# A two-block token mixer on one core: slot buffers moved by 96 bytes, four small moves between GpSimd and VectorE around a recurrence, and a longer lead of gates in the merge behind it

## The chip, the cores and the metric

The kernel runs on one core of a Trainium2 chip. The metric is the device time of one execution in microseconds. Three executions of the kernel before took 3236.25, 3236.37 and 3238.22 us; their median is 3236.37 us.

## The reference, cut to what matters

Four layers are applied one after the other to 512 tokens of width 1024 in float32: two layers of a first block, then two of a second. What matters here is the second block:

```
h = rmsnorm(x, pre_norm_g)
proj = h @ w_in
y_b = attention(...) * silu(z_b)
y_c = rg_lru(x_c, ...) * silu(z_c)            # 1280 channels
y_a = gmlp(...) * silu(z_a)
merged = sigmoid(g_a)*(y_a @ w_proj_a) + sigmoid(g_b)*(y_b @ w_proj_b) + sigmoid(g_c)*(y_c @ w_proj_c)
x = x + rmsnorm(merged @ w_out, post_norm_g)

rg_lru:  xc = conv4(x_c) + b
         r, i = sigmoid(blockdiag(xc, w_a) + b_a), sigmoid(blockdiag(xc, w_x) + b_x)   # 16 blocks of 80
         a = exp(-8 r softplus(-lam));  h_t = a_t h_{t-1} + sqrt(1 - a_t^2) * i_t * xc_t
```

## The kernel before, in words

**Arithmetic.** Every float32 matrix product is made of three products of fp32r halves: each operand is split into a high part (a rounded copy, made by ScalarE) and a low part (the rest, made by VectorE). `mm3` (lines 322 to 324) issues high times high, high times low, low times high. Most of these are 128x128 stationary by 512 columns moving.

**Weights.** All weights lie in HBM in the order in which they are used, as chunks of 128x1024. SyncE loads pairs of chunks into `raw`; `Stream._split` makes `whi` (ScalarE, line 179) and `wlo` (VectorE, line 180) from them, four chunks ahead of their use, in rings of seven.

**Activations.** The normalised input lies in two fixed tiles `hh` and `hl`. Everything else of 128x512 lies in 48 slots of 2048 bytes, which the trace calls `s`; `Slots.t` takes the slot that has been free the longest. `projT` makes one 128x512 output tile: eight blocks of a weight against `hh`/`hl` (24 matmuls), or as many as a list of slot pairs has. In `out_proj`, `tok_proj` and the attention the slots or `hh` are the stationary operand and the weights move.

**Where the buffers lie.** The tiles of a partition are laid one behind the other: `ident` (512 bytes), `pv` (2880), `half` (rounded up to 32), `hh` and `hl` (16384 each), the seven `whi` and seven `wlo` (4096 each), two `raw` (8192 each), the pool `small`, and the 48 slots. From `hh` to the end of `raw` each size is a multiple of 4096. The pool `small` holds, each tile rounded up to 32 bytes, 24 tiles of 32 bytes, 3 of 96, 3 of 64, 3 of 512, one of 256 and one of 192: 3232 bytes, which is 25 times 128 and 32.

**The recurrence (`lru`).** Ten tiles m of 128 channels. An iteration takes the gate weights of tile m+1 (`gate_weights`), makes the convolution of tile m+3 (`conv`, lines 1123 to 1130), copies rows that a block of 80 has outside its tile into a packed tile with DMAs (`pack`, line 1146, on the queues of GpSimd and SyncE), in four iterations (`ZPOS`: 4, 6, 7, 8) makes a projection z, and makes the two gates (`gates`). For six of the ten tiles the packed rows stand as high, low, high, so that one matmul of 96 rows (line 1170) does what otherwise takes three; it needs 32 rows of low weights beside the high ones, and the small copy on line 1160 puts them there: two per such tile, 24 in both layers. Behind the gates comes the product of the gate i with xc (line 1177). `scan` (lines 1185 to 1199) runs in pieces between these steps, at each `tick`: exponentials and square roots on ScalarE, a product (1196) and the scan itself (1197) on VectorE. After the tenth tile the remaining z projections follow, and for each tile silu(z) (lines 941, 942), its product with h (1238, or 1248 for the last two) and the split of the result (306, 307).

**The merge.** `merge` computes two gate tiles (`gate(0)`, `gate(1)`) ahead, and then, for each of eight outputs m, the projection of the branch's result, its product with the gate and the sum into `acc` (lines 683, 688), and `gate(m + 2)`.

**Order.** All of it is one program order written by hand: each engine runs its instructions in the order of the code. Each instruction waits only for what it reads and for buffers that it overwrites.

Of the kernel before, what the change touches and what calls it, by code (L numbers as in the profile page):

```python
# [8 lines left out]
F32 = mybir.dt.float32  # L9
F32R = mybir.dt.float32r  # L10
AF = mybir.ActivationFunctionType
ALU = mybir.AluOpType
# [5 lines left out]
KD = D // 128  # L18
# [15 lines left out]
E_U, E_V, E_ZA, E_CQ, E_CKV, E_KR, E_ZB, E_XC, E_ZC, E_GA, E_GB, E_GC = (  # L34
    0, 1024, 2048, 3072, 3456, 3712, 3776, 4800, 6080, 7360, 8384, 9408)

LW = 1280
NLT = LW // 128
# [41 lines left out]
def lru_rows(m):  # L80
    rows = [128 * k + i for k, r0, r1 in lru_outside(m) for i in range(r0, r1)]
    return tuple(rows * 3 if 3 * len(rows) <= 128 else rows)
# [27 lines left out]
class Slots:  # L110
    def __init__(self, pool, n, tag):
        self.pool, self.tag = pool, tag
        self.free_ = deque(range(n))
        self.where = {}
        self.low = n
        self.cnt = 0
# [121 lines left out]
class Kernel:  # L238
    def __init__(self, nc, tc, ctx, aps, total):
        self.nc, self.tc = nc, tc  # L240
        self.x_in, self.w, self.pv_in, self.rows, self.gmw, self.cst, self.out = aps
        fixed = ctx.enter_context(tc.tile_pool(name="fixed", bufs=1))
        self.wp = ctx.enter_context(tc.tile_pool(name="wp", bufs=RING))
        self.rawp = ctx.enter_context(tc.tile_pool(name="rawp", bufs=RAW))
        self.sm = ctx.enter_context(tc.tile_pool(name="small", bufs=6))
        self.s = Slots(ctx.enter_context(tc.tile_pool(name="slots", bufs=1)), NSLOT, "s")
        self.p = Slots(ctx.enter_context(tc.tile_pool(name="psum", bufs=1, space=bass.MemoryType.PSUM)), 8, "p")
        self.ws = Stream(self, total)
        self.ident = fixed.tile([128, 128], F32, tag="ident", name="ident")
        self.pv = fixed.tile([128, PV["n"]], F32, tag="pv", name="pv")  # L250
        self.half = fixed.tile([128, 4], F32, tag="half", name="half")
        self.hh = fixed.tile([128, KD, S], F32R, tag="hh", name="hh")
        self.hl = fixed.tile([128, KD, S], F32R, tag="hl", name="hl")
        self.xd = tc.dram_tile((S, D), F32, name="xd")
        self.h_op = [Op(self.hh[:, k, :], self.hl[:, k, :]) for k in range(KD)]
        self.lanes = {}
        self.x_src = self.x_in
        self.pend = None
        self.ht = {}
        self.pre = {}  # L260
        self.x = {}
# [399 lines left out]
        out[h] = self.split(sg[h])  # L661
        yield

    def merge(self, l, wg, cg, wy, ops, acc, n_br, last):

        nc, s, p = self.nc, self.s, self.p
        out, sgs = {}, {}

        def gate(m):
            pg = self.projT(wg, l, cg + 128 * m)  # L670
            sgs[m] = s.t()
            nc.scalar.activation(sgs[m][:], pg[:], AF.Sigmoid)  # L672
            p.f(pg)
            self.tick()

        gate(0)
        gate(1)
        if callable(ops):
            ops = ops()
        for m in range(KD):  # L680
            sg = sgs.pop(m)
            py = self.projT(wy, l, 128 * m, op=ops)
            nc.vector.tensor_tensor(sg[:], py[:], sg[:], op=ALU.mult)  # L683
            p.f(py)
            if n_br == 0:
                acc[m] = sg
            else:
                nc.vector.tensor_tensor(acc[m][:], acc[m][:], sg[:], op=ALU.add)  # L688
                s.f(sg)
                if last:  # L690
                    out[m] = self.split(acc.pop(m))
            self.tick()
            if m + 2 < KD:
                gate(m + 2)
        for o in ops:
            s.f(o.hi, o.lo)
        return out
# [402 lines left out]
    def lru(self, l):  # L1100
        nc, s, p = self.nc, self.s, self.p
        tt = nc.vector.tensor_tensor
        xc, op = {}, {}
# [30 lines left out]
        rr, ii, pk = {}, {}, {}  # L1134
# [17 lines left out]
        def gate_weights(m):  # L1152

            n = len(lru_rows(m))
            for nm in ("lru_w_a_2", "lru_w_x_2"):
                a = ws.take(128, (nm, l, 128 * m, 128 * m))
                hi, lo = ws.take(128, (nm, l, lru_rows(m), 128 * m))
                if n % 3 == 0 and n <= 96:
                    k = slice(n // 3 * 2, n)
                    nc.vector.tensor_copy(hi[k], lo[k].bitcast(F32))  # L1160
                gw[nm, m] = (a, (hi, lo))

        def gates(m):
            n, tiles = pk.pop(m)
            for nm, bias, dst in (("lru_w_a_2", "lba", rr), ("lru_w_x_2", "lbx", ii)):
                a, (hi, lo) = gw.pop((nm, m))
                ps = p.t()
                self.mm3(ps[:], a, (op[m].hi[:], op[m].lo[:]), True, False)
                if len(tiles) == 1:
                    nc.tensor.matmul(ps[:], hi[0:3 * n], tiles[0][0:3 * n, :], start=False, stop=True)  # L1170
                else:
                    self.mm3(ps[:], (hi[0:n], lo[0:n]), (tiles[0][0:n, :], tiles[1][0:n, :]), False, True)
                t = s.t()
                nc.scalar.activation(t[:], ps[:], AF.Sigmoid, bias=self.col(bias, l, m))
                p.f(ps)
                dst[m] = t
            nc.gpsimd.tensor_tensor(ii[m][:], ii[m][:], xc[m][:], op=ALU.mult)
            o = op.pop(m)
            s.f(xc.pop(m), o.hi, o.lo, *tiles)
            self.tick()  # L1180
# [26 lines left out]
        pack(1)  # L1207
        pz, sz = {}, {}
        gate_weights(0)
        for m in range(NLT):  # L1210
            if m + 1 < NLT:
                gate_weights(m + 1)
            if m + 3 < NLT:
                conv(m + 3)
                pack(m + 2)
                if m + 3 == NLT - 1:
                    pack(NLT - 1)
            if m in ZPOS:
                z = len(sz) + len(pz)
                ps = self.projT("w_in_2", l, E_ZC + 128 * z)  # L1220
                if m < 8:
                    sz[z] = self.silu(ps)
                else:
                    pz[z] = ps
                self.tick()
            gates(m)
            if m == 3:
                self.lane("scan", scan(range(4)))
        self.drain("scan")
        self.lane("scan", scan(range(4, NLT)))  # L1230
        ops = []
        nz = len(sz) + len(pz)
        for z in range(nz, NLT):
            pz[z] = self.projT("w_in_2", l, E_ZC + 128 * z)
            self.tick()
            for m in range(len(ops), z - 1):
                t = sz.pop(m) if m in sz else self.silu(pz.pop(m))
# [8 lines left out]
        for t in rest:  # L1246
            m = len(ops)
            tt(t[:], t[:], h[m][:], op=ALU.mult)
            s.f(h.pop(m))
            ops.append(self.split(t, eng=nc.gpsimd if m == NLT - 2 else None))  # L1250
        return ops

    def gmlp(self, l):
# [67 lines left out]
    def block2(self, l, last=False):  # L1321
        s = self.s
        c = self.mla_down(l)
        zb = []
        for h in range(3):
            ps = self.projT("w_in_2", l, E_ZB + 128 * h)
            if h == 0:
                self.tick()
            zb.append(self.silu(ps))
            if h:  # L1330
                self.tick(3)
        self.drain("mla")
        self.mla(l, c, zb)

        def yb():
            return [z if isinstance(z, Op) else self.split(z) for z in zb]

        acc = {}
        self.merge(l, "w_in_2", E_GB, "w_proj_b_2", yb, acc, 0, False)
        yc = self.lru(l)  # L1340
        self.merge(l, "w_in_2", E_GC, "w_proj_c_2", yc, acc, 1, False)
        ya = self.gmlp(l)
        self.x_load()
        merged = self.merge(l, "w_in_2", E_GA, "w_proj_a_2", ya, acc, 2, True)

        def done(k):
            s.f(merged[k].hi, merged[k].lo)

        self.out_proj("w_out_2", l, KD, merged.__getitem__, done, ("post2", l), ("pre2", 1), True, last=last)
# [155 lines left out]
```

## Time and profile before

| | us |
|---|---|
| median of the three runs | 3236.37 |
| the profiled execution | 3238.38 |
| its span, first to last instruction | 3236.5 |
| TensorE busy | 3181.7 (98%) |
| VectorE busy | 1867.2 (58%) |
| ScalarE busy | 1191.5 (37%) |
| GpSimd busy | 255.9 (8%) |

Busy time is a sum over the whole span. TensorE is busy nearly always, but a matmul is pipelined: its recorded duration (about 390 ns for 512 columns) is longer than the distance from its start to the next one's, so the speed of a stretch is read from how many matmuls it holds. The mean granted TensorE clock is 0.994 of full speed. The recurrence of the second block's first layer ends at about 2078 us of the span, that of its second layer at about 2868 us.

### The profile page before, as it was taken

The page shows a single profiled execution, that of the slowest core. Times are in us where ns is not written, and L with a number is a line of the kernel's source. Part 1 is how long each engine was busy: PE and PEld are TensorE (multiplying, and loading weights), DVE is VectorE, ACT ScalarE, POOL GpSimd, SP SyncE. Part 2 cuts the span into 40 slices and gives each one's busy share as a digit, 9 for nine tenths or more (in the row PEclk, how much of TensorE's full clock was granted, in tenths as well). Part 3 has the DMA queues.
Part 4 walks back from the last instruction along what each step waited for, and adds up shares of the span by engine and source line. Part 5 has one row for each costly group of instructions (what it writes and reads, how often), then busy time and mean ns, then how long its engine had stood idle before and what let it go on. Part 6 is the DMA issues. An engine that isn't in the chain of part 4 may idle for free. (4 is left out here: it accounts for less than half of the span.)

```text
span 3236.5 us, 36908 instructions
## 1 busy us (share of the span) xinstructions
PE 3181.7 (98%) x14808; PEld 2650.7 (82%) x14808; DVE 1867.2 (58%) x2729; ACT 1191.5 (37%) x1798; POOL 255.9 (8%) x362
## 2 busy tenths in 40 slices
PE   8999999999999999999999999999999999999998
PEld 7888888888888888888888887788888888778886
DVE  5687556663568755666358536635446844663643
ACT  4222343332422234333345526512234543632222
POOL 2000010000200001000010002200002001210000
PEclk9999999999999999999999999999999999999999
DMA  5222322232422232223222224322333213332221
GB/s 194 92 97 91 130 90 93 101 113 102 153 92 98 91 130 79 104 93 115 104 104 93 78 95 125 112 104 91 108 121 124 78 67 120 98 124 104 91 104 72
DMA packets 62540, 337.98 MB, mean 104 GB/s; under 512 B 10305, under 2 KB 10433, under 8 KB 27553
## 3 DMA queue, kind: packets, MB, share of 16 engines
q1 hardware_dynamic: 49984, 302.54, 26.5%
q0 software_dynamic: 11232, 31.08, 3.3%
q8 instruction: 116, 1.90, 0.2%
q10 hardware_dynamic: 1152, 2.01, 0.2%
q14 instruction: 56, 0.45, 0.0%
HBM read 310.68 MB, written 8.39 MB: 99 GB/s over the span
## 5 line engine op out<-in xcount | busy, mean ns | idle before, releaser
L322 PE MATMUL p<-hh,whi 128*128 128x512 f32 (+1 forms) x2752 | 1052.7, 383 | 1.6 <-ACT whi L179 1.6
L324 PE MATMUL p<-hh,wlo 128*128 128x512 f32 (+1 forms) x2752 | 1048.6, 381 | 1.5 <-DVE wlo L180 1.5
L323 PE MATMUL p<-hl,whi 128*128 128x512 f32 (+1 forms) x2752 | 1048.4, 381 | 0.0
L180 DVE TENSOR_TENSOR wlo<-raw,whi 128x1024 fp32r<-128x1024 f32 x544 | 675.7, 1249 | 522.0 <-ACT whi L179 520.8
L179 ACT ACTIVATE whi<-raw 128x1024 fp32r<-128x1024 f32 x544 | 562.7, 1052 | 287.8 <-PE p L324 197.6
L322 PEld LDWEIGHTS p<-hh,whi 128*128 128x128 f32 x2752 | 521.0, 189 | 99.6 <-ACT whi L179 2.0
L324 PEld LDWEIGHTS p<-hh,wlo 128*128 128x128 f32 x2752 | 520.0, 189 | 100.5 <-DVE wlo L180 1.8
L323 PEld LDWEIGHTS p<-hl,whi 128*128 128x128 f32 x2752 | 520.5, 189 | 96.8
L323 PE MATMUL p<-s,whi 128*128 128x512 f32 (+1 forms) x768 | 306.1, 399 | 2.4 <-POOL s L307 2.4
L322 PE MATMUL p<-s,whi 128*128 128x512 f32 (+1 forms) x768 | 305.9, 398 | 1.8 <-ACT s L306 1.8
L324 PE MATMUL p<-s,wlo 128*128 128x512 f32 (+1 forms) x768 | 305.7, 398 | 0.0
L323 PE MATMUL p<-wlo,s 128*128 128x512 f32 x640 | 254.1, 397 | 0.0
L322 PE MATMUL p<-whi,s 128*128 128x512 f32 x640 | 253.7, 396 | 0.0
L324 PE MATMUL p<-whi,s 128*128 128x512 f32 x640 | 252.3, 394 | 0.0
L306 ACT ACTIVATE s<-s 128x512 fp32r<-128x512 f32 x168 | 103.2, 627 | 363.6 <-DVE s L688 133.7
L672 ACT ACTIVATE s<-p 128x512 f32<-128x512 f32 x96 | 57.3, 597 | 468.6 <-PE p L324 468.6
L812 DVE SCALAR_TENSOR_TENSOR s<-p,pv,s 128x511 f32<-128x511 f32 (+1 forms) x176 | 131.8, 749 | 122.3 <-ACT s L809 119.2
L683 DVE TENSOR_TENSOR s<-p,s 128x512 f32<-128x512 f32 x96 | 66.3, 691 | 203.6 <-PE p L324 203.5
L566 DVE SCALAR_TENSOR_TENSOR s<-s,pv,s 128x511 f32<-128x511 f32 (+14 forms) x240 | 176.1, 734 | 5.7
L323 PEld LDWEIGHTS p<-s,whi 128*128 128x128 f32 (+1 forms) x768 | 145.5, 189 | 37.8 <-POOL s L307 3.9
L322 PEld LDWEIGHTS p<-s,whi 128*128 128x128 f32 (+1 forms) x768 | 145.0, 189 | 35.8 <-ACT s L306 2.7
L324 PEld LDWEIGHTS p<-s,wlo 128*128 128x128 f32 (+1 forms) x768 | 145.5, 189 | 34.5
(187 smaller groups left out, 3077.5 us busy)
## 6 DMA issues: line engine op xcount, KB each, us to landing
raw<-in_w_dram SPq DMA_DIRECT2D x272, 1024.0 KB, 4.8
s<-in_rows_dram POOLq DMA_DIRECT2D x32, 256.0 KB, 3.5
s<-s POOLq DMA_DIRECT2D x96, 64.0 KB, 2.5
xd<-s SPq DMA_DIRECT2D x24, 256.0 KB, 2.0
s<-xd POOLq DMA_DIRECT2D x24, 256.0 KB, 3.3
s<-s SPq DMA_DIRECT2D x88, 64.0 KB, 2.7
s<-in_cst_dram POOLq DMA_DIRECT2D x16, 256.0 KB, 3.8
s<-in_x_dram POOLq DMA_DIRECT2D x8, 256.0 KB, 5.8
```

The lines of the kernel that those rows point to most:

```text
L179: nc.scalar.activation(hi[:], src, AF.Copy)
L180: nc.vector.tensor_tensor(lo[:], src, hi[:].bitcast(F32), op=ALU.subtract)
L306: self.nc.scalar.activation(hi[:, :n], t[:, :n], AF.Copy)
L322: mm(ps, a[0], b[0], start=first, stop=False)
L323: mm(ps, a[0], b[1], start=False, stop=False)
L324: mm(ps, a[1], b[0], start=False, stop=last)
L566: nc.vector.scalar_tensor_tensor(c[:, sh:], glu[:, :S - sh], w(k), c[:, sh:], op0=ALU.mult, op1=ALU.add)
L672: nc.scalar.activation(sgs[m][:], pg[:], AF.Sigmoid)
L683: nc.vector.tensor_tensor(sg[:], py[:], sg[:], op=ALU.mult)
L812: nc.vector.scalar_tensor_tensor(t[:, sh:], ps[:, :S - sh], w(k), t[:, sh:], op0=ALU.mult, op1=ALU.add)
```

## The change

Six edits. (1) A tile of 24 floats is taken first of all in the pool `small` and never used; it moves everything behind it, the rest of `small` and all slots, by 96 bytes. (2) The small copy of low weight rows goes from VectorE to GpSimd. (3) The product of gate i with xc goes from GpSimd to VectorE. (4) Of the last two result splits of each recurrence, the one of tile 8 goes from GpSimd to VectorE; the splits of tiles 0 to 7 stay on GpSimd. (5) `merge` gets a parameter for the number of gates that it computes ahead, 2 unless told otherwise; (6) the merge behind the recurrence is called with 4.

```diff
         self.sm = ctx.enter_context(tc.tile_pool(name="small", bufs=6))
+        self.sm.tile([128, 24], F32, tag="shift", name="shift", bufs=1)
...
-    def merge(self, l, wg, cg, wy, ops, acc, n_br, last):
+    def merge(self, l, wg, cg, wy, ops, acc, n_br, last, lead=2):
...
-        gate(0)
-        gate(1)
+        for m in range(lead):
+            gate(m)
...
-            if m + 2 < KD:
-                gate(m + 2)
+            if m + lead < KD:
+                gate(m + lead)
...
                 if n % 3 == 0 and n <= 96:
                     k = slice(n // 3 * 2, n)
-                    nc.vector.tensor_copy(hi[k], lo[k].bitcast(F32))
+                    nc.gpsimd.tensor_copy(hi[k], lo[k].bitcast(F32))
...
-            nc.gpsimd.tensor_tensor(ii[m][:], ii[m][:], xc[m][:], op=ALU.mult)
+            tt(ii[m][:], ii[m][:], xc[m][:], op=ALU.mult)
...
-            ops.append(self.split(t, eng=nc.gpsimd if m == NLT - 2 else None))
+            ops.append(self.split(t))
...
-        self.merge(l, "w_in_2", E_GC, "w_proj_c_2", yc, acc, 1, False)
+        self.merge(l, "w_in_2", E_GC, "w_proj_c_2", yc, acc, 1, False, lead=4)
```

## Rows read from the trace of the kernel before

**Rows 1.** The page, busy time of each engine.
```profile
PE 3181.7 (98%) x14808; PEld 2650.7 (82%) x14808; DVE 1867.2 (58%) x2729; ACT 1191.5 (37%) x1798; POOL 255.9 (8%) x362
```

**Rows 2.** Waits of PE: who waited for whom, us in total, times, longest.
```profile
PE p L1170 <- DVE whi L1160: 10.5, 2, 5.3
...
PE p L323 <- POOL s L307: 2.4, 3, 0.9
```

**Rows 3.** Busy time by stretch: length, engines (instructions), clock granted to PE, DMA share, GB/s.
```profile
2017.70:2023.00 5.30, 0.21 (x1) 0.00 (x0) 5.25 (x6) 1.23 (x3) 2.95 (x2) 0.82 0.54 198
2023.00:2027.80 4.80, 4.77 (x11) 3.85 (x12) 1.90 (x3) 2.90 (x4) 1.28 (x1) 0.50 0.51 160
2075.00:2079.00 4.00, 2.17 (x8) 0.98 (x7) 3.30 (x6) 2.68 (x5) 2.23 (x4) 1.00 0.26 111
2079.00:2082.40 3.40, 3.40 (x10) 2.64 (x9) 3.20 (x3) 3.30 (x4) 1.51 (x3) 0.51 0.75 207
2807.30:2812.80 5.50, 0.17 (x2) 0.01 (x1) 5.45 (x7) 1.39 (x3) 3.10 (x2) 0.70 0.54 191
2812.80:2816.30 3.50, 3.50 (x8) 2.80 (x9) 1.29 (x2) 1.66 (x3) 0.21 (x1) 0.50 0.37 66
2864.20:2867.50 3.30, 1.59 (x5) 0.49 (x3) 2.60 (x5) 1.83 (x4) 1.52 (x2) 1.00 0.48 204
2867.50:2874.40 6.90, 6.22 (x15) 4.87 (x16) 6.66 (x7) 4.56 (x6) 3.17 (x6) 0.51 0.65 208
```

**Rows 4.** Timeline of DVE in the first wait: start, us, instruction, [idle before].
```profile
2016.40 3.41 DVE L180 TENSOR_TENSOR wlo<-raw,whi 128x1024 fp32r<-128x1024 f32 x2
...
2022.76 0.35 DVE L1160 CAST whi<-wlo 32x128 fp32r<-32x128 f32 x2
```

**Rows 5.** Timeline of POOL ahead of and in that wait.
```profile
2011.01 1.51 POOL L1146 DMA_DIRECT2D s<-s  x3 [5.46 <-ACT s L1129]
...
2016.90 1.82 POOL L1177 TENSOR_TENSOR s<-s,s 128x512 f32<-128x512 f32 x1 [2.23 <-ACT s L1174]
```

**Rows 6.** Groups by line and shape, POOL: count, busy us, mean ns, idle before.
```profile
L307 POOL TENSOR_TENSOR s<-s,s 128x512 fp32r<-128x512 f32 x18 | 29.1, 1625 | 72.4 <-ACT s L306 62.3 <-issue 10.1
L1177 POOL TENSOR_TENSOR s<-s,s 128x512 f32<-128x512 f32 x20 | 28.2, 1408 | 56.1 <-ACT s L1174 56.0
```

**Rows 7.** The same for DVE.
```profile
L307 DVE TENSOR_TENSOR s<-s,s 128x512 fp32r<-128x512 f32 x150 | 102.7, 698 | 61.9 <-ACT s L306 61.4
...
L688 DVE TENSOR_TENSOR s<-s,s 128x512 f32<-128x512 f32 x64 | 44.3, 692 | 2.2
...
L1160 DVE CAST whi<-wlo 32x128 fp32r<-32x128 f32 x24 | 4.7, 216 | 0.4
```

**Rows 8.** Two stretches of pure 512-column matmuls: on `hh`, and in a projection from slots.
```profile
600.00:660.00 60.00, 60.00 (x267) 49.69 (x266) 37.33 (x45) 21.19 (x27) 2.21 (x4) 1.00 0.37 119
760.00:820.00 60.00, 60.00 (x259) 48.28 (x258) 19.93 (x23) 17.13 (x26) 0.94 (x2) 1.00 0.25 91
```

**Rows 9.** Groups by line and shape, PE; moving operand first, stationary second.
```profile
L322 PE MATMUL p<-hh,whi 128*128 128x512 f32 x2496 | 978.1, 392 | 0.0
...
L322 PE MATMUL p<-s,whi 128*128 128x512 f32 x752 | 299.6, 398 | 1.8 <-ACT s L306 1.8
...
L322 PE MATMUL p<-whi,s 128*128 128x512 f32 x640 | 253.7, 396 | 0.0
...
L322 PE MATMUL p<-whi,hh 128*128 128x512 f32 x192 | 74.8, 390 | 0.0
...
L323 PE MATMUL p<-hl,whi 128*128 128x256 f32 x256 | 73.6, 288 | 0.0
...
L1026 PE MATMUL p<-ident,s 128*128 128x128 f32 x160 | 20.6, 274 | 2.5 <-DVE s L1015 2.4
...
L999 PE MATMUL p<-s,s 128*128 128x256 f32 x32 | 9.1, 283 | 0.0
```

**Rows 10.** Timeline of DVE at the end of the first recurrence.
```profile
2077.59 1.33 DVE L307 TENSOR_TENSOR s<-s,s 128x512 fp32r<-128x512 f32 x1 [0.70 <-ACT s L306]
```

## The prediction

> **What bounds the kernel now.** I read the page's busy times first. TensorE is busy for 3181.7 of 3236.5 us [rows 1], so only two things can move the end: time in which TensorE stands still or runs at the lower clock, and the speed of its matmuls. The other engines count only where TensorE waits for them.
>
> Then TensorE's waits. Two belong to this change: line 1170 waits twice, up to 5.3 us, for the small copy on VectorE, and the merge's first projection waits for result splits [rows 2]. The busy times by stretch give their whole price, in both layers [rows 3]. In the four waiting stretches TensorE idles 5.30 - 0.21 = 5.09, 5.50 - 0.17 = 5.33, 4.00 - 2.17 = 1.83 and 3.30 - 1.59 = 1.71 us, and 6.90 - 6.22 = 0.68 in the last row: 14.6 us. After each wait the granted clock is 0.50 or 0.51 of full speed, 1.2 GHz of 2.4, until the next stretch at full speed. Half of the busy time there is lost: 4.77/2 + 3.50/2 + 0.49 x 3.40 + 0.49 x 6.22 = 2.39 + 1.75 + 1.67 + 3.05 = 8.9 us. Together 23.5 us hang on the recurrence and the merge behind it.
>
> Last, the matmuls. Two stretches of 60 us, without a wait and at full clock, hold 267 matmuls on `hh` and 259 in a projection from slots [rows 8]: 224.7 against 231.7 ns each (cut ends are counted alike in both), 7 ns more where a slot is an operand. The grouped durations agree: 398 ns for a moving slot against 392 for `hh`, 396 for a stationary slot against 390 [rows 9]. So it is not the role of the operand but that it lies in a slot.
>
> **The change part by part.**
>
> *The small copy.* The 5.09 and 5.33 us are VectorE's backlog: in the first wait it is busy 5.25 of 5.30 us [rows 3], with weight splits of 3.41 us for two and more, and reaches the copy only at 2022.76 [rows 4]. TensorE had used the low half of the same chunk on line 324 before it stood still, so the data were there. On GpSimd the two copies stand behind the pack DMAs that end at 2011.01 + 1.51 = 2012.5 [rows 5]; the product that follows there goes to VectorE. The trace shows no copy on GpSimd. Below, the price is VectorE's own 216 ns [rows 7]; above, GpSimd's product of four times the columns and partitions, 1408 ns [rows 6]. I take 0.4 us, nearer the small one. Even at 1.41 two copies end at 2015.3, before 2017.7, when TensorE asks. Cover: 2.4 us; without it the copy's excess is TensorE's. So 10.4 us of idle time and 4.1 us of half clock go. GpSimd does 24 copies, at most 34 us in total, in stretches where it is mostly idle; the only thing queued behind them there is the next pack's DMAs, whose rows are used an iteration later.
>
> *The product with xc.* VectorE gets 20 x 0.69 us (line 688 has the same form [rows 7]) and loses 24 x 0.22: 8.6 us more over two recurrences. Against that, products on GpSimd and weight splits on VectorE overlapped in the wait [rows 4, 5], and there the product took 1.82 us against a mean of 1.41 [rows 5, 6]; a VectorE split beside one on GpSimd took 1.33 us against a mean of 0.70 [rows 10, 7]. Each holds up the other, and with the product on VectorE this goes. I cost it at nothing. The new wait: VectorE now waits for the gate's sigmoid, with scan pieces, the next convolution and weight splits queued behind it. TensorE would feel that only through a late split, and the splits run four chunks ahead, some 20 us at 24 matmuls of 0.227 us per chunk. VectorE is behind TensorE there, not ahead [rows 3], so the sigmoid is done when it arrives. If that cover went, the 8.6 us would be the loss.
>
> *The split of tile 8.* 1.62 us on GpSimd become 0.70 on VectorE [rows 6, 7], twice. About nothing here, since the next edit covers it.
>
> *Lead of 4.* Two more gates, 48 matmuls of 0.227 us, 10.9 us of work that needs no result of the recurrence, stand ahead of the projection that waits. The waits there (1.83 + 1.71 + 0.68) and their half clock (1.67 + 3.05) go: 8.9 us. The gates only change places: their sigmoids, weight chunks and SyncE loads come earlier by two gates, and none is added. What is late next: with the first wait gone TensorE arrives at the merge about 7 us earlier; VectorE's chain of exponentials, scan, product and split starts from the last gates and so moves too, by some 5 us. The cover of 10.9 us exceeds the old wait of about 3 us by more than the difference. The last four projections then run without gates between them, and VectorE has two products of 0.69 us and some weight splits to do per projection of 30 matmuls, 7 us.
>
> Of the 23.5 us I take 22 as gained, leaving 1.5 for what remains of the chain.
>
> *The 96 bytes.* By the sizes, slots lie 32 bytes past the place of `hh`, `whi` and `wlo` modulo 128, since only `small`, 3232 = 25 x 128 + 32 bytes, is no multiple of it. With 96 more it is 3328 = 26 x 128, and slots, `hh` and weights agree modulo 128 (and 256, not 512). What the rows allow: where both operands agree (`hh` with weights) matmuls are fast; where they don't (slots with weights) 6 to 7 ns are added. Where a slot meets a slot, at 256 columns, 283 ns stand against 288 for `hh` with weights [rows 9]: no surcharge. So the cause that fits all four is that stationary and moving operand start differently within a line of the memory, and the shift removes it. It would then hold for 3 x 752 + 3 x 640 = 4176 matmuls (lines 323 and 324 have the counts of line 322 [rows 9]); at 6.5 ns that is 27 us. The bounds: 0 where the place modulo 128 isn't the cause, and 31 us at 7.5 ns above. Below, the other sign (the third rival). `ident` agrees with the slots now and won't after: 496 transposes, the 160 of line 1026 [rows 9] and five groups like it, at most 7 ns each, 3.5 us. They are short and paced by other things; I take 1.
>
> The Trainium skill (TensorE: Matmul & The Clock Gate, step-by-step in part 2) says the array has two independent read ports and that loading the next weights doesn't steal bandwidth from the running matmul. By that rule no address could matter, and the sum would be without the 27 us; the 267 against 259 matmuls don't settle it, as they show a difference and not its cause.
>
> **Sum.** From the profiled execution's 3238.38 us: less 22, less 27, plus 1, is 3190. The median of the three runs is 2.0 us under the profiled execution, so 3188.
>
> **The rivals.**
>
> *The shift does nothing, or little.* The slots also lie all beyond the weights, and everything fast lies ahead of them; distance and place modulo 128 can't be told apart in this trace, nor 256 from 512. Against it: slot with slot is not slow. Then 3238.4 - 22 - 2 = 3214.
>
> *The gain of the recurrence comes back.* TensorE reaches the merge earlier, but VectorE's chain doesn't follow, because it is full there (3.30 of 4.00 and 3.20 of 3.40 us [rows 3]) and now has the products. Against it: the overlap with GpSimd goes. Then half of 22 stays: 3188 + 11 = 3199.
>
> *Slower.* It isn't the agreement but each slot's own start that costs: slots at a multiple of 32 that is none of 64 would take one line more per stream. `hh` and the weights already lie so and are fast, which speaks against it. Price: another 7 ns on each of the 4176, 29 us, against 22 gained: 3236.4 + 29 - 22 = 3243. It decides from 22/4176 = 5.3 ns a matmul.
>
> **How the numbers follow.** Forecast 58%, its own range 3180 to 3196. Shift without effect or with a part of it 24% (3200 to 3216), the gain coming back 12% (about 3199), slower 5%, about the same 1%. The range reaches from 3178 (31 us and all 23.5) to 3217, where the first rival ends; out of it lie the slower case and some misses. About 0.2%, 6.5 us, is what a measurement of this kernel can tell from no change. Faster by more: 0.58 + 0.24 + 0.12 less a little for mishaps, 0.92; the same 0.03; slower 0.05.
>
> **What would show it.** Steps right: no wait of line 1170; no stretch at half clock in the recurrence or behind it; a stretch like 760 to 820 us, long before the recurrence, with about 267 matmuls in 60 us and 390 ns for `p<-s,whi` and `p<-whi,s`. Wrong: 259 there (first rival); waits on weight splits or line 307 near the end of the recurrence (second); fewer than 259 (third).

## The result, and the profile after

The changed kernel takes 3188.1 us (median; 3187.5 to 3191.4), the kernel before 3236.3 in the same runs: a ratio of 0.9855 (95% interval 0.984 to 0.9871), 48.2 us less. The forecast was 3188.0. The profiled execution took 3187.5 us, its span 3185.7.

The page of the changed kernel, busy time of each engine ([rows 1] of before). Lines from 246 on have moved by one, so that the three matmuls of a projection stand on L323 to L325, the small copy on L1161, the product on L1178.

```profile
span 3185.7 us, 36912 instructions
...
PE 3139.7 (99%) x14808; PEld 2637.0 (83%) x14808; DVE 1862.8 (58%) x2727; ACT 1192.0 (37%) x1798; POOL 236.0 (7%) x364
```

TensorE runs the same 14808 matmuls in 42.0 us less busy time, and its idle time falls from 54.8 to 46.0 us. Its waits after the change, longest first (us in total, times, longest):

```profile
PE p L416 <- DVE s L400: 17.2, 11, 10.8
PE p L324 <- DVE wlo L180: 5.5, 4, 1.9
PE p L323 <- ACT whi L179: 4.3, 3, 1.8
PE p L1027 <- DVE s L1016: 2.7, 2, 1.3
PE p L325 <- DVE wlo L180: 2.6, 3, 1.5
```

No line waits for the small copy or for a split of the recurrence's results any more; both waits of [rows 2] are gone. What is left in the recurrences and at their ends is waits for weight splits and 0.8 us for the DMAs of `pack`. The busy times by stretch of the changed kernel (length, then PE, PEld, DVE, ACT and POOL with their instructions, granted clock, DMA share, GB/s) run from the end of the first recurrence into the merge, and then through the end of the second recurrence; they answer to [rows 3]:

```profile
1980.00:2000.00 20.00, 19.70 (x86) 15.75 (x85) 17.57 (x22) 10.90 (x17) 5.26 (x11) 1.00 0.46 146
2000.00:2054.00 54.00, 54.00 (x240) 44.54 (x239) 39.43 (x48) 32.18 (x47) 13.25 (x8) 1.00 0.26 95
2054.00:2061.00 7.00, 5.59 (x24) 4.01 (x23) 5.08 (x7) 4.90 (x7) 2.20 (x4) 1.00 0.49 166
2061.00:2100.00 39.00, 39.00 (x174) 32.30 (x173) 16.05 (x16) 12.65 (x16) 1.08 (x2) 1.00 0.46 157
2766.00:2826.00 60.00, 59.36 (x261) 48.59 (x260) 44.31 (x53) 37.40 (x54) 14.22 (x11) 1.00 0.27 92
2826.00:2833.00 7.00, 4.72 (x20) 3.26 (x19) 5.08 (x7) 4.59 (x7) 2.20 (x4) 1.00 0.57 174
```

The clock stays at 1.00 in all these stretches, where before it was granted 0.50 or 0.51 in four of [rows 3]. TensorE stands still for 7.00 - 5.59 = 1.41 and 7.00 - 4.72 = 2.28 us at the two ends.

The matmuls: a stretch of 60 us that holds nothing but 512-column matmuls of weights on slots, first in the kernel before, then in the changed one (with PE alone):

```profile
740.00:800.00 60.00, 60.00 (x259) 1.00 0.30 105
```

```profile
740.00:800.00 60.00, 60.00 (x266) 1.00 0.25 88
```

That is the pace of `hh` in [rows 8]. The groups by shape of the changed kernel say the same, against 398 and 396 ns in [rows 9]:

```profile
L323 PE MATMUL p<-hh,whi 128*128 128x512 f32 x2496 | 974.4, 390 | 0.0
L323 PE MATMUL p<-s,whi 128*128 128x512 f32 x752 | 293.7, 391 | 2.6 <-ACT whi L179 2.6
...
L323 PE MATMUL p<-whi,s 128*128 128x512 f32 x640 | 250.1, 391 | 0.0
...
L1027 PE MATMUL p<-ident,s 128*128 128x128 f32 x160 | 20.6, 274 | 2.7 <-DVE s L1016 2.7
```

Below I also use the distance from the start of one 512-column matmul to the start of the next of the same kind, worked out over the trace's list of matmuls: 227.0 ns for `hh` with weights in both kernels; before, 233.9 with a slot as moving and 233.4 as stationary operand; after, 227.2 and 226.9.

### The profile page after: what moved, and what is told of

It reads as the page before. It is cut to its first block, busy times and chain, and to the rows that moved or that the text cites. A ratio compares the mean times of both kernels' runs of the same rounds, so it can differ in the third digit from the quotient of the medians.

```text
span 3185.7 us, 36912 instructions
## 1 busy us (share of the span) xinstructions
PE 3139.7 (99%) x14808; PEld 2637.0 (83%) x14808; DVE 1862.8 (58%) x2727; ACT 1192.0 (37%) x1798; POOL 236.0 (7%) x364
## 5 line engine op out<-in xcount | busy, mean ns | idle before, releaser
L323 PE MATMUL p<-hh,whi 128*128 128x512 f32 (+1 forms) x2752 | 1048.8, 381 | 1.6 <-ACT whi L179 1.6
L325 PE MATMUL p<-hh,wlo 128*128 128x512 f32 (+1 forms) x2752 | 1045.2, 380 | 1.5 <-DVE wlo L180 1.5
L325 PEld LDWEIGHTS p<-hh,wlo 128*128 128x128 f32 x2752 | 518.6, 188 | 99.3 <-DVE wlo L180 1.8
L323 PEld LDWEIGHTS p<-hh,whi 128*128 128x128 f32 x2752 | 518.9, 189 | 98.5 <-ACT whi L179 2.0
L323 PE MATMUL p<-s,whi 128*128 128x512 f32 (+1 forms) x768 | 300.2, 391 | 3.1 <-ACT whi L179 2.6
L325 PE MATMUL p<-s,wlo 128*128 128x512 f32 (+1 forms) x768 | 299.2, 390 | 1.0 <-DVE wlo L180 1.0
L324 PE MATMUL p<-s,whi 128*128 128x512 f32 (+1 forms) x768 | 299.4, 390 | 0.4 <-DMA s<-s 0.4
L323 PE MATMUL p<-whi,s 128*128 128x512 f32 x640 | 250.1, 391 | 0.0
L325 PE MATMUL p<-whi,s 128*128 128x512 f32 x640 | 249.2, 389 | 0.0
L323 PEld LDWEIGHTS p<-s,whi 128*128 128x128 f32 (+1 forms) x768 | 144.3, 188 | 34.1 <-ACT whi L179 3.5
L325 PEld LDWEIGHTS p<-s,wlo 128*128 128x128 f32 (+1 forms) x768 | 144.1, 188 | 32.0 <-DVE wlo L180 1.9
```

Source lines behind the costliest of these rows:

```text
L323: mm(ps, a[0], b[0], start=first, stop=False)
L324: mm(ps, a[0], b[1], start=False, stop=False)
L325: mm(ps, a[1], b[0], start=False, stop=last)
```

## The experiments

Theory: two gains that add. The shift lets slot and weights start at the same place, worth about 27 us; the edits of the recurrence and the merge remove waits and the half clock behind them, about 22 us. Rivals: the place itself or the distance counts and not the agreement; of the recurrence's edits only one works, or its gain comes back.

Where in the kernel a run gains or loses can be read from the matmuls: every kernel issues the same 14808, in the same order outside the merges behind the recurrences, so the time between the starts of two of them compares from trace to trace. The table at the end of this section has it for the two recurrences with their merges and for the starts of the two layers.

**e1_shift_only: the kernel before with the shift alone.**

```
+        self.sm.tile([128, 24], F32, tag="shift", name="shift", bufs=1)
```

> The kernel before with the 96 bytes alone. Theory (the surcharge comes from stationary and moving operand starting at different places modulo 128): 4176 slot matmuls fall by 6.5 to 7 ns each, 27 to 29 us; with what waits take back I expect 3206 to 3211 us. Rival (the shift as such does little, and the other edits made most of the 48 us): 3230 us or more. The recurrence's waits on the small copy and its half clock stay as before.

3208.7 us, ratio 0.9919 (0.9905 to 0.9934): 27.2 us less. The window of slot matmuls holds 266, and the wait for the copy is there as before:

```profile
740.00:800.00 60.00, 60.00 (x266) 1.00 0.25 88
```

```profile
PE p L1171 <- DVE whi L1161: 10.3, 2, 5.3
```

By the distances, 2256 matmuls with a moving slot x 6.7 ns and 1920 with a stationary one x 6.5 are 27.6 us. The shift's part is thus the matmuls and nothing else.

**e2_no_shift: the changed kernel without the shift** (the line above taken out).

> The changed kernel without the 96 bytes. Theory: the recurrence's edits are worth 17 to 22 us, so 3215 to 3219 us, and a slot matmul costs 7 ns more than one on hh, as before. Rival (most of the gain is the other edits): under 3200 us.

3218.8 us, ratio 0.9949 (0.9932 to 0.9965): 17.1 us less than before. 258 matmuls in the window:

```profile
740.00:800.00 60.00, 60.00 (x258) 1.00 0.30 105
```

The two halves alone add up to 44.3 us and together give 48.2; the last section comes back to the rest.

**e3_all_at_zero: the changed kernel with 32 bytes ahead of `hh`**, so that, by the sizes and counted from the start of `ident`, `hh`, the weights, the slots and `ident` all start at a multiple of 128.

```
+        fixed.tile([128, 8], F32, tag="pad", name="pad")
```

> The changed kernel with 32 bytes more ahead of hh, so that hh, the weights and the slots all start at a multiple of 128, and ident too. Theory of agreement: as fast as the changed kernel, 3186 to 3189 us, perhaps 1 us better as ident agrees. Theory of the place itself (32 past a multiple of 64 is the fast place, a multiple of 128 the slow one): every 512-column matmul slow, some 12,000 of them at 7 ns, 84 us more, about 3270 us. Theory of distance (what lies beyond the weights is slow): no change against the kernel after.

3189.7 us, ratio 0.986 (0.9845 to 0.9875), as the changed kernel; slot matmuls at 227 ns. The place itself doesn't matter. `ident` neither gains nor loses by its place: its transposes start every 109 ns here, in the changed kernel and in the one before, where it agrees with the slots modulo 256 (here it agrees modulo 128 only).

**e4_shift_32: the kernel before with 32 bytes in place of 96.**

```
+        self.sm.tile([128, 8], F32, tag="shift", name="shift", bufs=1)
```

> The kernel before with the slots moved by 32 bytes instead of 96: slots at 32, hh and weights at 96 modulo 128, so they agree modulo 64 and 32 but not modulo 128. If agreement modulo 64 is enough: as the shift of 96 alone, 3206 to 3211 us. If it has to be modulo 128: as before, 3236 us. If the surcharge grows with the distance in bytes: between these or above.

3230.4 us, ratio 0.9983 (0.9973 to 0.9992). A moving slot still takes 233.4 ns, a stationary one 230.5 on the mean: 1920 x 2.9 ns + 2256 x 0.5 = 6.7 us, and 5.5 were measured. The window has

```profile
740.00:800.00 60.00, 60.00 (x264) 1.00 0.29 103
```

so part of the surcharge went here, without agreement modulo 128.

**e5_weights_moved: the changed kernel with 32 bytes between `hl` and the weights.** Weights and slots then start alike modulo 256, `hh` and `hl` 32 bytes before them.

> The changed kernel with 32 bytes more behind hl: weights and slots now start at a multiple of 128, hh and hl stay at 96 past it. Theory of agreement: slot matmuls stay fast, and the 7488 + 576 512-column matmuls of hh and hl with weights, some 8,060, take 6.7 ns more each: 54 us, so about 3242 us. Theory of distance or of the buffer itself: no change, 3188 us.

3237.9 us, ratio 1.0004 (0.9994 to 1.0015): all the gain is gone, 49.8 us over the changed kernel. Slots with weights keep 227; the window of `hh` falls from 267 to

```profile
600.00:660.00 60.00, 60.00 (x259) 1.00 0.29 97
```

`hh` isn't a slot, and hasn't moved: only the weights beside it have. At 233.3 ns, 7488 + 576 matmuls x 6.4 ns are 51.6 us. So it is agreement of the two operands, whoever they are.

**e9_shift_224: the kernel before with 224 bytes**, 128 more than 96. Slots and weights agree modulo 128 but not modulo 256.

```
+        self.sm.tile([128, 56], F32, tag="shift", name="shift", bufs=1)
```

> The kernel before with the slots moved by 224 bytes in place of 96: slots, hh and weights then start alike modulo 128 but not modulo 256 (they differ by 128 there). Agreement modulo 128 is what counts: slot matmuls of 512 columns start every 227 ns as with 96 bytes, and the time is 3208 to 3210 us against 3236. Agreement modulo 256 is needed: 230 to 234 ns stay, and the time is 3230 to 3236.

3232.7 us, ratio 0.999 (0.9981 to 1.0): nearly nothing, and the slot matmuls stay at 232.9 and 232.7 ns:

```profile
740.00:800.00 60.00, 60.00 (x259) 1.00 0.28 104
```

Agreement modulo 128, on which my sum rested, is not enough. All runs together, by how far the start of the weight lies past that of the other operand, modulo 256 (worked out from the sizes of the tiles):

```
apart   run (operands)                      start to start, moving / stationary slot
  0     after, e1, e10 (slot, weight)       227.2 / 226.9
  0     e3 (slot, weight)                   227.3 / 226.9
  0     e5 (slot, weight)                   227.8 / 226.9
 32     e5 (hh, weight)                     233.3 / 233.3 (hh moving / stationary)
 64     e4 (slot, weight)                   233.4 / 230.5
 96     before, e2 (slot, weight)           233.9 / 233.4
128     e9 (slot, weight)                   232.9 / 232.7
```

**e6_copy_back: the changed kernel with the small copy on VectorE.**

```
-                    nc.gpsimd.tensor_copy(hi[k], lo[k].bitcast(F32))
+                    nc.vector.tensor_copy(hi[k], lo[k].bitcast(F32))
```

> The changed kernel with the small copy back on VectorE. Theory: the copy's place behind VectorE's backlog made the two long waits of the block gates, so they come back; shorter by what the product's move took from the backlog, 2 to 5 us each, with half clock behind: 3194 to 3202 us. Rival (the product on GpSimd, which held VectorE up, made the backlog): no wait over 1 us, under 3191 us.

3200.1 us, ratio 0.9887 (0.9872 to 0.9901): 12.0 us more than the changed kernel. The wait is back, and behind it the half clock (waits of PE, then the stretch behind the wait with all engines):

```profile
PE p L1171 <- DVE whi L1161: 7.6, 2, 3.9
```

```profile
2004.80:2011.60 6.80, 4.95 (x12) 3.90 (x13) 5.18 (x8) 3.08 (x4) 0.00 (x0) 0.50 0.53 216
```

The other layer has a second stretch at half clock, of 3.4 us. That this comes to 7.6 + 4.95/2 + 3.4/2 = 11.8 us, near the 12.0, is chance. TensorE comes later to the merge here, and the 3.7 us of waits for weight splits at the two ends are gone, which leaves 8.1; between the same matmuls the recurrences with their merges take 7.2 us more than in the changed kernel. Another 6.1 us lie at the starts of the layers, where this run has a stretch of 6.8 us at half clock in each layer and the changed kernel has none; the rest of the kernel takes 0.7 less, and the two profiled executions differ by 12.7.

**e7_product_back: the changed kernel with the product on GpSimd.**

```
-            tt(ii[m][:], ii[m][:], xc[m][:], op=ALU.mult)
+            nc.gpsimd.tensor_tensor(ii[m][:], ii[m][:], xc[m][:], op=ALU.mult)
```

> The changed kernel with the product of gate i and xc back on GpSimd. Theory: a copy on GpSimd must stay behind one product at most, so no long wait of the block gates; within 3 us of the changed kernel, either way. Rival (moving the product is what freed VectorE): the weight splits come later by about 1 us for each of ten tiles, and TensorE waits at the end of the recurrence for 5 us or more in each layer: over 3196 us. Scans and products of VectorE (means 1224 and 695 ns) go back to some 1380 and 840.

3189.3 us, ratio 0.9852 (0.9838 to 0.9867): no difference. The copy now stands behind products on GpSimd and takes longer (823 ns on the mean, 480 in the changed kernel), and TensorE waits for it, but shortly and at full clock:

```profile
PE p L1171 <- POOL whi L1161: 2.2, 2, 1.2
```

**e8_lead_2: the changed kernel with a lead of 2.**

```
-        self.merge(l, "w_in_2", E_GC, "w_proj_c_2", yc, acc, 1, False, lead=4)
+        self.merge(l, "w_in_2", E_GC, "w_proj_c_2", yc, acc, 1, False)
```

> The changed kernel with a lead of two gates as before. Theory: TensorE arrives about 5 us earlier than before at a merge that had waited 2 to 3 us, so it waits there for the result splits, some 5 to 8 us in each layer with half clock behind: 3198 to 3206 us. Rival (the split on VectorE had cured it): 3190 us or less.

3202.0 us, ratio 0.9894 (0.9878 to 0.9911): 13.9 us more than the changed kernel. The projections wait for the result splits, on ScalarE now as well as on GpSimd, and run on at half clock (waits, then stretches):

```profile
PE p L323 <- ACT s L307: 5.7, 4, 2.3
...
PE p L324 <- POOL s L308: 1.8, 2, 0.9
```

```profile
2053.50:2063.70 10.20, 8.84 (x18) 5.23 (x18) 7.88 (x10) 6.66 (x10) 3.30 (x5) 0.50 0.58 186
...
2835.00:2842.00 7.00, 6.54 (x13) 4.10 (x14) 5.17 (x6) 5.57 (x8) 2.20 (x4) 0.51 0.52 151
```

The wait of 7.5 us is larger than the one of [rows 2] and [rows 3], 3.5 to 4.2: with the copy's wait gone TensorE arrives earlier. So without the lead a good part of the copy's gain would have come back here: between the same matmuls the recurrences with their merges take 12.4 us more than in the changed kernel, the starts of the layers 2.4. The split of tile 8, on VectorE here too, does not cure it.

**v1_ahead_lead5: towards a better version.** In the changed kernel ScalarE's order at the end of the first recurrence is (timeline: start, us, instruction, idle before):

```profile
2054.67 0.63 ACT L307 ACTIVATE s<-s 128x512 fp32r<-128x512 f32 x1 [1.46 <-DVE s L1249]
2056.73 0.63 ACT L307 ACTIVATE s<-s 128x512 fp32r<-128x512 f32 x1 [1.43 <-DVE s L1249]
2057.27 1.04 ACT L179 ACTIVATE whi<-raw 128x1024 fp32r<-128x1024 f32 x1
```

The weight split at 2057.27 stands behind two result splits that wait for VectorE's last products; TensorE waits for it. The edit issues two more chunks' splits ahead of those, and leads by 5:

```
+        ws.ahead(ws.cur + AHEAD + 2)
         rest = [self.silu(pz.pop(m)) for m in range(len(ops), NLT)]
...
-        self.merge(l, "w_in_2", E_GC, "w_proj_c_2", yc, acc, 1, False, lead=4)
+        self.merge(l, "w_in_2", E_GC, "w_proj_c_2", yc, acc, 1, False, lead=5)
```

> The kernel after, with the weight splits of one more chunk than usual taken ahead of the last gated branch's rest, and a merge that leads by 5 gates. Theory: the 6 us in which TensorE still waits for weight splits at the end of the recurrence (2057 and 2829 us) are VectorE's backlog behind the scan; with more splits done ahead of it they go, and the time is 3182 to 3186. Rival: VectorE has no spare time before it either, and the backlog and its waits only move to an earlier or a later place: 3187 to 3190.

3185.4 us, ratio 0.9843 (0.9828 to 0.9858). TensorE is busy throughout both ends (PE alone):

```profile
2054.00:2061.00 7.00, 7.00 (x32) 1.00 0.64 222
2826.00:2833.00 7.00, 7.00 (x33) 1.00 0.60 203
```

The span is 3183.2 us against 3185.7. The ratios' intervals overlap, so the times alone don't separate the two kernels; that the 3.7 us of waits are gone the trace shows. Between the same matmuls the recurrences with their merges are 5.1 us shorter than in the changed kernel, and the starts of the layers 3.2 us longer, with a stretch of 3.4 us at half clock in each.

**e10_shift_352_ahead: two edits that show in different stretches.** Slots moved by 352 bytes, 256 more than 96; and of v1 only the earlier weight splits, at a lead of 4.

```
-        self.sm.tile([128, 24], F32, tag="shift", name="shift", bufs=1)
+        self.sm.tile([128, 88], F32, tag="shift", name="shift", bufs=1)
...
+        ws.ahead(ws.cur + AHEAD + 2)
```

> The kernel after with two edits that show in different views. The slots are moved by 352 bytes, 256 more than 96: with 224 bytes, where slots and weights agreed modulo 128 and differed by 128 modulo 256, the slot matmuls stayed slow, so the agreement must be modulo 256, and 352 must then do what 96 does: a start every 227 ns, 267 matmuls from 760 to 820 us, and no change of the time. Were it something else of the 96 bytes, 232 to 234 ns come back and the time rises by 25 to 30 us. And of the two edits of the version that led by 5 only the earlier weight splits are kept, with a lead of 4: if these alone took away the waits for weight splits at the end of the recurrence, 3184 to 3187 us; if it was the lead of 5, the waits at 2057 and 2829 us stay and the time is 3188 to 3190.

3186.4 us, ratio 0.9854 (0.9837 to 0.987), span 3182.6. The window has 266 again, and both ends are free of waits:

```profile
740.00:800.00 60.00, 60.00 (x266) 1.00 0.25 88
...
2054.00:2061.00 7.00, 7.00 (x33) 1.00 0.61 231
2826.00:2833.00 7.00, 7.00 (x32) 1.00 0.52 199
```

So 352 does what 96 does: the period is 256 bytes. (In this kernel the operands agree modulo 512 too, in the changed one they don't; that gives nothing more.) And the earlier weight splits alone remove the last waits, and shorten the recurrences with their merges by the same 5.1 us; the lead of 5 isn't needed.

**v2_split_dve: the changed kernel with the recurrence's result splits on VectorE** and one chunk's weight split taken ahead.

```
-                ops.append(self.split(t, eng=nc.gpsimd))
+                ops.append(self.split(t))
...
+        ws.ahead(ws.cur + AHEAD + 1)
```

> The kernel after, with the splits of the recurrence's results that are on GpSimd moved to VectorE, and one chunk's weight split taken ahead of the rest. Theory: a weight split beside a GpSimd split takes 2.25 us in place of 1.24 for a pair, so without GpSimd's splits VectorE's backlog falls and the 6 us of waits shrink: 3183 to 3187. Rival: VectorE gets 14 more splits of 0.7 us, which is more than it saves, and the waits grow: 3189 to 3195.

3190.6 us, ratio 0.9857 (0.9842 to 0.9872). Not better: TensorE's waits for weight splits come to 13.1 us (12.4 in the changed kernel), the largest part now

```profile
PE p L325 <- DVE wlo L180: 6.0, 5, 1.8
...
PE p L324 <- DVE wlo L180: 5.5, 4, 1.9
...
PE p L323 <- ACT whi L179: 1.6, 1, 1.6
```

Whether VectorE's added splits or the one chunk less than in e10 does that, this run can't say.

**The same matmuls, run by run.** Time between the same two matmuls in the profiled executions, us against the kernel before. There, the starts of the layers are 1630 to 1690 and 2430 to 2490 us, the recurrences with their merges 1900 to 2250 and 2690 to 3040. The last column has the stretches at half clock at the starts of the layers, first and second, us long.

```
run      starts of   recurrences   the rest     all   half clock at the
         layers      with merges                      starts of layers
before     0.0          0.0          0.0        0.0   6.8, 3.4
e1        +0.4         -4.7        -23.3      -27.6   6.8, 3.4
e2        +0.9        -20.1         +0.1      -19.0   6.8, 6.8
after     -4.3        -23.7        -22.7      -50.6   none
e6        +1.8        -16.5        -23.4      -38.0   6.8, 6.8
e7        -2.3        -25.8        -21.5      -49.6   3.4, none
e8        -1.8        -11.3        -23.0      -36.2   3.4, 3.4
v1        -1.1        -28.8        -23.1      -52.9   3.4, 3.4
e10       -2.7        -28.8        -22.3      -53.7   none, 3.4
v2        -2.7        -23.1        -23.6      -49.4   3.4, none
```

## Why the prediction was right

*What bounds the kernel.* TensorE alone, through its waits, its clock and the speed of its matmuls. The runs agree: what each of the two halves moved is found again in these.

*The 96 bytes, -27.* Measured: 27.2 alone (e1), 30.7 on top of the other edits (e2 against after). The size and the sign of the cause, two operands that start differently, were right: e5 slows `hh` without touching it. But the step "slots, `hh` and weights agree modulo 128" named the wrong modulus. By it e9 would have gained 27 us, and it gained 3.9. The rows that I used can't tell 128 from 256. The prediction left only 256 against 512 open; the number came out because 96 bytes give agreement by 128 and by 256, and that was luck. One of the rows was no evidence at all: slot with slot was read at 256 columns, and at 256 columns e5 shows no surcharge for operands that start 32 bytes apart either, 285 ns against 288 in [rows 9]:

```profile
L325 PE MATMUL p<-hl,whi 128*128 128x256 f32 x256 | 73.0, 285 | 0.0
```

The first rival (the distance) and the third (a slot's own start) are out by e3, e5 and e10.

*The Trainium skill's rule* (TensorE: Matmul & The Clock Gate, step-by-step in part 2), two independent read ports and a weight load that takes no bandwidth from the running matmul, would have left 3214 us; the runs disagree with what I took from it: an address alone moves these matmuls from 227 to 233 ns and the kernel by 27 us (e1) and 50 us (e5). What in the chip does it, no run here shows.

*`ident`, +1.* Measured nothing: 274 ns before, where `ident` agrees with the slots, and after, where it doesn't. In these runs only 512-column matmuls show the surcharge.

*The small copy.* Forecast 0.4 us on GpSimd, between 0.216 and 1.41 [rows 6, 7]; it took 0.48 (groups of GpSimd in the changed kernel, with the splits that stayed there first):

```profile
L308 POOL TENSOR_TENSOR s<-s,s 128x512 fp32r<-128x512 f32 x16 | 26.5, 1665 | 90.3 <-ACT s L307 90.3
...
L1161 POOL CAST whi<-wlo 32x128 fp32r<-32x128 f32 x24 | 10.8, 480 | 0.1
```

The timeline has two of them from 1995.05 on, right behind the pack DMAs, and the matmuls that use them don't wait:

```profile
1993.53 1.52 POOL L1147 DMA_DIRECT2D s<-s  x3 [4.96 <-ACT s L1130]
1995.05 0.79 POOL L1161 CAST whi<-wlo 32x128 fp32r<-32x128 f32 x2
```

*The product, at nothing.* Right, and mainly for the reason given. VectorE's groups in the changed kernel, then in e7 with the product on GpSimd:

```profile
L180 DVE TENSOR_TENSOR wlo<-raw,whi 128x1024 fp32r<-128x1024 f32 x544 | 671.7, 1242 | 476.7 <-ACT whi L179 475.5 <-DMA s<-s 0.3
...
L1198 DVE TENSOR_TENSOR_SCAN s<-s,s 128x512 f32<-128x512 f32 x20 | 24.5, 1224 | 0.7
L1197 DVE TENSOR_TENSOR s<-s,s 128x512 f32<-128x512 f32 x20 | 13.9, 695 | 0.0
L1178 DVE TENSOR_TENSOR s<-s,s 128x512 f32<-128x512 f32 x20 | 13.5, 685 | 18.3 <-ACT s L1175 18.3
```

```profile
L180 DVE TENSOR_TENSOR wlo<-raw,whi 128x1024 fp32r<-128x1024 f32 x544 | 677.9, 1254 | 494.7 <-ACT whi L179 493.3 <-DMA s<-s 0.5
L1198 DVE TENSOR_TENSOR_SCAN s<-s,s 128x512 f32<-128x512 f32 x20 | 29.6, 1480 | 0.7
L1197 DVE TENSOR_TENSOR s<-s,s 128x512 f32<-128x512 f32 x20 | 15.9, 794 | 2.5 <-ACT s L1194 2.5
```

The 20 products cost VectorE 13.5 us, and these three other groups become shorter by 6.2 + 5.1 + 2.0 = 13.3. But the prediction also held that the sigmoid is done when VectorE arrives, and that was wrong: VectorE waits 18.3 us for it. TensorE feels none of it, so the sum was not hurt.

*Copy and lead together, -22.* By the times, 20.6 on top of the shift (e1 against after) and 17.1 without it (e2). Neither number is the recurrence alone. Between the same matmuls, the recurrences with their merges lost 19.0 us on top of the shift and 20.1 without it; most of the remaining difference lies at the starts of the layers. So the term was some 2 to 3 us too large. I had left 1.5 us for what remains, and the trace shows 1.41 + 2.28 = 3.7 us of waits for weight splits at the two ends: 23.5 - 3.7 = 19.8. That is the place where the second rival looked, at a third of its price of 11. Its mechanism is real, as e8 shows, but the lead of 4 covers it. Taken away alone, the copy's move costs 7.2 us there (e6) and the lead 12.4 (e8), 19.6 against 19.0 for all; the whole times, 12.0 and 13.9, make it look as if the edits did not add, because the starts of the layers are in them. The split of tile 8 was not tried alone.

*What no term named.* The changed kernel also gains 4.3 us at the starts of the two layers, far from the edits, where the kernel before ran at half clock for 6.8 and 3.4 us. These 4.3 us are of the profiled executions, whose spans differ by 50.7 us where the medians differ by 48.2; how much of them is in the medians the record doesn't say. Without them, the 27.2 of the shift and the 19.0 to 20.1 of the recurrence would leave 3189 to 3190 us from 3236.3. The forecast holds by its own terms, then, but that it met 3188.1 so closely is luck.

One figure of the prediction's range was wrong: 31 and 23.5 us off 3236.4 leave 3181.9 and not 3178. Neither the forecast nor the rivals used it.

## What to carry to other kernels

Read matmul pace by kind of operand pair before asking about waits: a difference of 3% that follows an operand and not a shape may come from its address, and padding so that moving and stationary operand start alike modulo 256 bytes costs nothing to try. When the rows leave two explanations and the change satisfies both, the number is safe and the reason isn't; a second padding that satisfies only one of them settles it. When two runs differ, compare the time between the same matmuls before crediting the whole difference to the edit: in e6 a clock that fell far away made about half of it. A wait that is taken off TensorE shows up at the next hand-over unless that one gets slack too, and its price is the idle time and the half clock behind it.

## What the runs showed that was not expected

*Half clock at the start of a layer.* In the kernel before, each layer of this block starts with a stretch at half clock, far from the change, behind waits for weight splits of together 2.4 us in the first layer and 2.7 in the second. In the changed kernel the same waits are 2.8 and 2.7 us and the clock stays up; with the shift alone it falls again. The stretches behind the waits in the kernel before (both layers), then in the first layer of the changed one and of e1:

```profile
1656.00:1663.00 7.00, 6.36 (x23) 5.86 (x22) 5.85 (x15) 4.22 (x12) 0.62 (x2) 0.53 0.67 198
...
2448.00:2452.00 4.00, 4.00 (x17) 4.00 (x17) 2.86 (x6) 2.35 (x9) 0.56 (x1) 0.61 0.88 238
```

```profile
1642.00:1650.00 8.00, 6.70 (x40) 6.38 (x41) 6.85 (x12) 4.92 (x12) 2.04 (x2) 1.00 0.65 210
```

```profile
1643.00:1650.00 7.00, 6.24 (x21) 6.24 (x22) 5.69 (x17) 3.76 (x11) 0.64 (x2) 0.51 0.70 216
```

It is the place where the two halves of the change gain more together than alone: the starts of the layers give 4.3 us in the changed kernel, and cost 0.4 and 0.9 in e1 and e2. These 5.6 us are more than the 3.9 that are missing in the sum of the halves. It is not the profiled executions alone: all four of the changed kernel had a mean granted clock of 0.999, and those of e2 0.997 or 0.998, with no half clock left around its recurrences. But e7's trace has one such stretch, and v1's two, with the same edits ahead of that place; whether the clock falls there hangs on little, and what decides it is open.

*Part of the surcharge.* 64 bytes apart (e4), a stationary slot pays 3.6 ns and a moving slot 6.4. No run says why.
